# Transposing unscaled tokens by a product with a diagonal, in both RMS norms of a DeltaNet and MLP layer

## The chip, the cores and the metric

The kernel runs on one core of one Trainium2 chip. The metric is the time of one execution on the device in microseconds (us), as the median over several runs. A core has a matrix engine, TensorE (PE in the profile; PEld is its loading of weights), VectorE (DVE), ScalarE (ACT), GpSimd (POOL), and SyncE (SP), which here issues the transfers. Each engine works through its own queue of instructions in order, and semaphores order the engines among each other.

## The reference, cut to what matters

There is one layer of kind 0: a norm, a gated DeltaNet mixer, a residual add, a second norm, an MLP with squared ReLU, a residual add, and a final norm. The change touches the first two norms.

```
def rmsnorm(x, g):                                  # x: 1024 tokens x 1024
    y = x * rsqrt(mean(x * x, axis=-1) + 1e-6)      # one root for each token
    return y * g                                    # one gain for each column

h = x
h = h + gated_deltanet(rmsnorm(h, norm_mix_g), ...)   # (h @ w_in) -> conv, scan, ... -> @ w_out
h = h + square(relu(rmsnorm(h, norm_mlp_g) @ w1)) @ w2
out = rmsnorm(h, final_norm_g)
```

All data are 32-bit floats.

## The kernel before

The 1024 tokens are eight tiles of 128 (tokens on the partitions, 1024 columns free). A product with a weight matrix contracts over the columns, so the normed tokens are needed transposed, as `xT` for the mixer and `hT` for the MLP: 128 columns on the partitions for each of eight column blocks `kt`, tokens free. Both are kept as a high and a low half (`dh`, `dl`, a rounded value and what is left of it), since each big product is made of three products of 512 columns on rounded operands (lines 127 to 129, 824 to 826, 1080 to 1082, 1301 to 1303).

**First norm (lines 183 to 230).** For each tile, `norm_x` sums the squares (ACT or DVE, the squares go to a throw-away tile `junk`), adds the epsilon and takes the power -1/2 on POOL (lines 77 and 78), and scales the whole tile by its root in place (line 196; DVE for tiles 0 to 3, POOL for tiles 4 to 7). `turn_x` then transposes 128x128 blocks on TensorE against the identity (line 204) into eight PSUM tiles `tpx`, one for each `kt`, with four token tiles side by side in each. ACT writes the high half out of each and DVE the low half, both multiplied with the gain (lines 208 and 209). Tiles 0 to 3 (group 0) come first in the program; then `project_ab` (`pab`, a small product with `wab`) and the first window's products with the weights of key head 0 (`pk`, `half_of(0, 0)`). The squares of tiles 4 to 7 (group 1) are issued there, and their transposes after the first half of the second window (`half_of(1, 0)`, key head 1).

`tpv` (line 174) is the transpose of the small vectors (conv weights, gains), read from three small transfers into a tile `scr`; `pvec` is copied from it. Line 230 takes the exponential of `a_log`, eight numbers that a transfer (line 172) brings to all partitions; it is used much later, in `decays`.

**Second norm (lines 745 to 785, called at 833).** For each of the eight tiles of the output projection (products `pm`, lines 824 to 826), ACT sums the squares of the 1024 columns into `ss`, POOL takes the root, DVE multiplies the tile with root and gain into `hs` (line 751), and one tile later TensorE transposes `hs` (line 759) into two tiles `tpn`, out of which ACT and DVE write `hT` and sums that the MLP needs (`T1s`, `T2s`, `T4s`).

**Start of the MLP.** Each product of w1 with `hT` is done by a scheme of seven half-size products (`A11`, `S1` to `S4`, ... are sums of weight blocks; `T1`, `T2`, `T4` sums of `hT` blocks). Products 1 and 2 of the first three pairs come first (`p_0_1` to `p_2_2`), then `p_0_3`, `p_0_6`, `p_0_5`, ... `split_T` (lines 1021 to 1026) splits the T sums on ACT and DVE just before, under a higher priority; `wsplit` (line 83, `wh_S` in the trace) does the same for the weight sums.

The order on each engine is chosen by a list scheduler from priorities that follow the order of the program and from its own estimates of time; `tc.issue_after(x)` makes it hold instructions back until `x` has been issued. Tiles of one tag share a fixed number of buffers (`bufs`), in turn.

Of the kernel before, what the change touches and what calls it, by code (L numbers as in the profile page):

```python
# [28 lines left out]
def trunk_kernel(  # L29
# [144 lines left out]
    nc.tensor.transpose(tpv[:, 0:105], pv, ident[0:105, 0:105])  # L174


    nc.vector.tensor_scalar(out=pvec[:, 0:96], in0=tpv[:, 0:96], scalar1=0.5, scalar2=0.0, op0=MUL, op1=ADD)
    nc.vector.tensor_scalar(out=pvec[:, 96:97], in0=tpv[:, 96:97], scalar1=-0.5, scalar2=0.0, op0=MUL, op1=ADD)
    nc.vector.tensor_copy(pvec[:, 97:105], tpv[:, 97:105])
    sx = small([2, NT])  # L180

    def norm_x(t, sq, sc):

        junk = gp.tile([P, D], F32, tag="V", name=f"junk_{t}", bufs=2)
        ss = sx[:, 0, t : t + 1]
        if sq == "act":
            nc.scalar.activation(junk, xts[t], AF.Square, scale=1.0 / 32, accum_out=ss)
        else:
            nc.vector.scalar_tensor_tensor(out=junk, in0=xts[t], scalar=1.0 / D, in1=xts[t], op0=MUL, op1=MUL, accum_out=ss)
        rsqrt_pool(sx[:, 1, t : t + 1], ss, 1)  # L190
        rs = sx[:, 1, t : t + 1]
        if sc == "act":
            nc.scalar.activation(xts[t], xts[t], AF.Copy, scale=rs)
        else:
            eng = nc.gpsimd if sc == "pool" else nc.vector
            eng.tensor_scalar(out=xts[t], in0=xts[t], scalar1=rs, scalar2=1.0, op0=MUL, op1=MUL)

    def turn_x(g, tags):

        tps = [(ps if tag == "gemm" else px).tile([P, 512], F32, tag=tag, name=f"tpx_{g}_{kt}", bufs=4 if tag == "gemm" else 2)  # L200
               for kt, tag in enumerate(tags)]
        for kt, tp in enumerate(tps):
            for j in range(4):
                nc.tensor.transpose(tp[:, j * P : j * P + P], xts[4 * g + j][:, kt * P : kt * P + P], ident)
# [3 lines left out]
            nc.scalar.activation(dh, tp, AF.Copy, scale=gk)  # L208
            nc.vector.scalar_tensor_tensor(out=dl, in0=tp, scalar=gk, in1=dh.bitcast(F32), op0=MUL, op1=SUB)
# [22 lines left out]
    def decays():  # L232
        tab = px.tile([P, 512], F32, tag="ch", name="tab", bufs=2)
        for t in range(NT):
# [31 lines left out]
        nc.gpsimd.affine_select(out=up, in_=up, pattern=[[1, P]], compare_op=ALU.is_ge, fill=0.0,  # L266
                                base=0, channel_multiplier=-1)
# [225 lines left out]
    def merge(p, Xs):  # L493
# [7 lines left out]
        for e, (X, Y) in both:  # L501
# [3 lines left out]
            nc.gpsimd.memset(Y[0:32, :, 32:64], 0.0)  # L505
# [239 lines left out]
    def norm_to_T(src, t, g_bc, hs, name):  # L745

        ss = gp.tile([P, 2], F32, tag="sso", name=f"ss_{name}", bufs=3)
# [614 lines left out]
```

## Time and profile before

| | |
|---|---|
| median of 3 runs | 1277.77 us (1276.76 to 1277.99) |
| the profiled execution, its own time | 1277.02 us |
| its span on the core | 1275.3 us |
| TensorE busy | 1245.9 us, 98% |
| VectorE, ScalarE, GpSimd busy | 928.6, 734.6, 382.4 us |

The span is what the profile shows between the first and the last instruction; 1.7 us of the execution's own time lie around it. Busy times of TensorE overlap from one product to the next, since they are pipelined, so the step from one start to the next is what a product costs in a full queue.

### The profile page before, as it was taken

Reading aid. Unit: us, or ns where it says so; the run is one execution under the profiler, and the core shown is the slowest. Engines: PE = TensorE matmul, PEld = TensorE weight load, DVE = VectorE, ACT = ScalarE, POOL = GpSimd, SP = SyncE. Lnnn points to the kernel's source line nnn. Section 1 sums busy time; section 2 is a strip of 40 time slices with the busy share of each in tenths; the row PEclk is TensorE's granted clock in tenths of the full one; section 3 lists DMA queues with packets and bytes.
Section 4 is the critical chain, followed back from the end, with each engine's and each line's share of the span. In section 5 each row is a group of like instructions: output and inputs, shape, how many; then the busy total and the mean of one; then the engine's idle time right before and its main releaser. Section 6 shows DMA issues by size and latency. Waiting matters only on the chain. (4 is left out here: it accounts for less than half of the span.)

```text
span 1275.3 us, 18776 instructions
## 1 busy us (share of the span) xinstructions
PE 1245.9 (98%) x6656; PEld 1024.5 (80%) x6656; DVE 928.6 (73%) x1739; ACT 734.6 (58%) x1578; POOL 382.4 (30%) x335
## 2 busy tenths in 40 slices
PE   7999999999999999999999999999999999999996
PEld 5788888888888888778877888888887788888885
DVE  5799689679957976755657555555557997877897
ACT  4682465554565445643366554554558787686765
POOL 6120122111211101202234233233215444526484
PEclk9999999999999999999999999999999999999999
DMA  5241222221212120331153433333307225233003
GB/s 185 78 111 50 51 63 63 59 63 50 71 51 63 51 51 24 110 99 51 50 161 111 141 99 105 127 100 105 128 17 279 91 82 164 78 100 133 1 1 132
DMA packets 103983, 113.04 MB, mean 89 GB/s; under 512 B 23465, under 2 KB 75858, under 8 KB 103890
## 3 DMA queue, kind: packets, MB, share of 16 engines
q1 hardware_dynamic: 103890, 111.86, 28.3%
q8 instruction: 52, 0.85, 0.3%
q14 instruction: 41, 0.34, 0.1%
HBM read 90.83 MB, written 21.00 MB: 88 GB/s over the span
## 5 line engine op out<-in xcount | busy, mean ns | idle before, releaser
L1302 PE MATMUL p<-hT 128*128 128x512 f32 x448 | 174.9, 390 | 2.8 <-DVE hT L977 2.8
L1303 PE MATMUL p<-hT 128*128 128x512 f32 x448 | 174.3, 389 | 0.0
L1301 PE MATMUL p<-hT 128*128 128x512 f32 x448 | 173.7, 390 | 0.0
L954 POOL TENSOR_TENSOR u<-u,u 128x1024 f32<-128x1024 f32 x48 | 123.0, 2581 | 149.3 <-ACT cp_T L976 45.1
L975 ACT CAST hT<-u 128x1024 fp32r<-128x1024 f32 x112 | 112.8, 1050 | 29.5 <-PE p L1302 27.6
L78 POOL TENSOR_TENSOR sso<-sso,cons 128x1 f32<-128x1 f32 x64 | 42.1, 657 | 264.4 <-DVE sso L596 264.3
L1302 PEld LDWEIGHTS p<-hT 128*128 128x128 f32 x448 | 84.1, 188 | 22.0 <-DVE hT L977 4.5
L1301 PEld LDWEIGHTS p<-hT 128*128 128x128 f32 x448 | 84.1, 188 | 18.3 <-ACT P L1319 0.6
L1303 PEld LDWEIGHTS p<-hT 128*128 128x128 f32 x448 | 84.1, 188 | 17.2
L1104 DVE TENSOR_TENSOR u<-u,p 128x512 f32<-128x512 f32 x61 | 41.8, 686 | 44.6 <-PE p L1082 44.5
L1231 DVE TENSOR_TENSOR oT<-oT,p 128x512 f32<-128x512 f32 x80 | 53.1, 677 | 12.8 <-PE p L1303 12.8
L127 PE MATMUL pg<-xT,wh_g 128*128 128x512 f32 x128 | 54.4, 425 | 0.0
L127 PE MATMUL pq<-xT,wh_q 128*128 128x512 f32 x128 | 53.9, 421 | 0.0
L127 PE MATMUL pv<-xT,wh_v 128*128 128x512 f32 x128 | 53.6, 419 | 0.0
L127 PE MATMUL pk<-xT,wh_k 128*128 128x512 f32 x128 | 53.1, 415 | 0.0
L129 PE MATMUL pg<-xT,wl_g 128*128 128x512 f32 x128 | 52.4, 409 | 0.0
L128 PE MATMUL pg<-xT,wh_g 128*128 128x512 f32 x128 | 51.6, 403 | 0.0
L129 PE MATMUL pv<-xT,wl_v 128*128 128x512 f32 x128 | 51.6, 403 | 0.0
L128 PE MATMUL pv<-xT,wh_v 128*128 128x512 f32 x128 | 51.5, 402 | 0.0
L128 PE MATMUL pk<-xT,wh_k 128*128 128x512 f32 x128 | 51.1, 399 | 0.0
L824 PE MATMUL pm<-wh_o,oh 128*128 128x512 f32 x128 | 50.7, 399 | 0.3 <-ACT wh_o L83 0.2
L129 PE MATMUL pk<-xT,wl_k 128*128 128x512 f32 x128 | 50.9, 397 | 0.0
(319 smaller groups left out, 3630.1 us busy)
## 6 DMA issues: line engine op xcount, KB each, us to landing
u<-in_mlp_w_dram SPq DMA_DIRECT2D x38, 512.0 KB, 4.3
u<-hd SPq DMA_DIRECT2D x28, 512.0 KB, 5.0
ra<-in_mlp_w_dram SPq DMA_DIRECT2D x26, 512.0 KB, 4.2
hd<-u SPq DMA_DIRECT2D x25, 256.0 KB, 4.1
hd<-c SPq DMA_DIRECT2D x20, 256.0 KB, 2.3
xt<-in_x_dram SPq DMA_DIRECT2D x8, 512.0 KB, 4.7
wr_k<-in_gdn_w_in_dram SPq DMA_DIRECT2D x16, 256.0 KB, 3.3
wr_q<-in_gdn_w_in_dram SPq DMA_DIRECT2D x16, 256.0 KB, 2.9
```

What stands on the lines that cost most here:

```text
L78: nc.gpsimd.tensor_tensor(out=dst, in0=src, in1=mhalf[:, :n], op=ALU.pow)
L127: nc.tensor.matmul(o, hi, act[:, 0, kt, s], start=(kt == 0), stop=False)
L128: nc.tensor.matmul(o, hi, act[:, 1, kt, s], start=False, stop=False)
L129: nc.tensor.matmul(o, lo, act[:, 0, kt, s], start=False, stop=(kt == KT - 1))
L824: nc.tensor.matmul(o, oh[k // 4][0][:, k % 4, :], wo[k][0][:, s], start=(k == 0), stop=False)
L954: (V if name in ("T1", "T3") else G).tensor_tensor(out=o, in0=a, in1=b, op=op)
L975: nc.scalar.copy(hi, t)
L1104: add = lambda out, x, y: V.tensor_tensor(out=out, in0=x, in1=y, op=ADD)
L1231: add = lambda eng, out, x: eng.tensor_tensor(out=out, in0=out, in1=x, op=ADD)
L1301: nc.tensor.matmul(o, hid(0, kt)[:, s], w(0, kt), start=(kt == 0), stop=False)
L1302: nc.tensor.matmul(o, hid(0, kt)[:, s], w(1, kt), start=False, stop=False)
L1303: nc.tensor.matmul(o, hid(1, kt)[:, s], w(0, kt), start=False, stop=(kt == g - 1))
```

## The change

Both norms no longer scale before the transpose. In the first norm, POOL's root of a tile goes into a diagonal matrix `dx[:, t]` (identity times root, 128x128), and the transposes are ordinary products of the raw tile with this diagonal: out = tile^T times diag(root). The diagonals are made on DVE for tiles 0 to 3 and on POOL for tiles 4 to 7. In the second norm, `hs` is the tile times the gain alone (two halves, each right behind its add), the squares are summed in two halves, and the product is with `diag[:, t]`.

The steps of the first four tiles are put in a fixed order by `issue_after` (tile 0, 1, then the copies of `pvec`, tile 2, 3; tile 3's squares half on ACT, half on DVE). Group 0 is turned token tile by token tile over all eight `kt`, no longer `kt` by `kt`; group 1 is interleaved with the products of window 1's first half instead of following it.

```diff
-    def norm_x(t, sq, sc):
+    def square_x(t, sq):
...
+        if sq != "dve":
+            nc.scalar.activation(junk[:, lo], xts[t][:, lo], AF.Square, scale=1.0 / 32, accum_out=ss)
+        if sq != "act":
+            return nc.vector.scalar_tensor_tensor(out=junk[:, hi], in0=xts[t][:, hi], scalar=1.0 / D, in1=xts[t][:, hi], op0=MUL, op1=MUL,
+                                                  accum_out=s2 if sq == "both" else ss)
+
+    def norm_x(t, eng, sq=None):
+
+        ss, rs, s2 = (sx[:, i, t : t + 1] for i in range(3))
+        nc.gpsimd.tensor_scalar(out=ss, in0=ss, scalar1=s2 if sq == "both" else 0.0, scalar2=EPS, op0=ADD, op1=ADD)
+        root = rsqrt_pool(rs, ss, 1, 0.0)
+        return root, eng.tensor_scalar(out=dx[:, t, :], in0=ident, scalar1=rs, scalar2=1.0, op0=MUL, op1=MUL)
...
-        for kt, tp in enumerate(tps):
-            for j in range(4):
-                nc.tensor.transpose(tp[:, j * P : j * P + P], xts[4 * g + j][:, kt * P : kt * P + P], ident)
+        for j in range(4):
+            t = 4 * g + j
+            for kt, tp in zip(kts, tps):
+                nc.tensor.matmul(tp[:, j * P : j * P + P], xts[t][:, kt * P : kt * P + P], dx[:, t, :], start=True, stop=True)
...
-    for t, (sq, sc) in enumerate((("act", "dve"), ("dve", "dve"), ("act", "dve"), ("act", "dve"))):
-        norm_x(t, sq, sc)
-
-    split(wab[:, :, 0:16], wab[:, :, 16:32], rab, "pool", "pool")
-    split(*wt0[0], raw0[0], "act")
-    split(*wt0[1], raw0[1], "pool", "pool")
-    turn_x(0, ["gemm"] * 4 + ["tp", "ch"] * 2)
+    square_x(0, "act")
+    square_x(1, "dve")
+    rooted, normed = norm_x(0, nc.vector)
+    with tc.issue_after(rooted.ins):
+        rooted, normed = norm_x(1, nc.vector)
+    with tc.issue_after(normed.ins):
...
+        square_x(2, "act")
+        squared = square_x(3, "both")
+    with tc.issue_after(squared.ins), tc.issue_after(rooted.ins):
+        norm_x(2, nc.vector)
+        rooted, normed = norm_x(3, nc.vector, "both")
+
+    with tc.issue_after(rooted.ins), tc.issue_after(normed.ins):
+        split(wab[:, :, 0:16], wab[:, :, 16:32], rab, "pool", "pool")
+        split(*wt0[0], raw0[0], "act")
+        split(*wt0[1], raw0[1], "pool", "pool")
+    turned = turn_x(0, range(KT), lambda kt: "gemm" if kt < 4 else ("tp", "ch")[kt % 2])
     project_ab(0)
     nc.scalar.activation(nea, nea, AF.Exp)
...
-    half_of(0, 0, plan[0])
-    for t, (sq, sc) in enumerate((("act", "pool"), ("dve", "pool"), ("act", "pool"), ("dve", "pool"))):
-        norm_x(4 + t, sq, sc)
-    half_of(1, 0, None)
-    turn_x(1, ["tp", "ch"] * 4)
+    with tc.issue_after(turned[0].ins), tc.issue_after(turned[1].ins):
+        half_of(0, 0, plan[0])
+        for t, sq in enumerate(("act", "dve", "act", "dve")):
+            square_x(4 + t, sq)
+            norm_x(4 + t, nc.gpsimd)
+    half_of(1, 0, [[lambda kt=kt: turn_x(1, [kt], lambda kt: ("tp", "ch")[kt % 2])] for kt in range(KT)])
...
-        nc.scalar.activation(hs, src, AF.Square, scale=1.0 / 32, accum_out=ss[:, 0:1])
-        rsqrt_pool(ss[:, 1:2], ss[:, 0:1], 1)
-        yield
-        nc.vector.scalar_tensor_tensor(out=hs, in0=src, scalar=ss[:, 1:2], in1=g_bc, op0=MUL, op1=MUL)
+        for n in range(2):
+            c = slice(n * 512, n * 512 + 512)
+            nc.scalar.activation(pt[n], src[:, c], AF.Square, scale=1.0 / 32, accum_out=ss[:, n : n + 1])
+            nc.vector.tensor_tensor(out=hs[:, c], in0=src[:, c], in1=g_bc[:, c], op=MUL)
+        nc.gpsimd.tensor_scalar(out=ss[:, 2:3], in0=ss[:, 0:1], scalar1=ss[:, 1:2], scalar2=EPS, op0=ADD, op1=ADD)
+        rsqrt_pool(ss[:, 3:4], ss[:, 2:3], 1, 0.0)
+
+        dg = diag[:, t, :]
+        nc.vector.tensor_scalar(out=dg, in0=ident, scalar1=ss[:, 3:4], scalar2=1.0, op0=MUL, op1=MUL)
+        yield
...
-                nc.tensor.transpose(tp[:, j * P : j * P + P], hs[:, kt * P : kt * P + P], ident)
+                nc.tensor.matmul(tp[:, j * P : j * P + P], hs[:, kt * P : kt * P + P], dg, start=True, stop=True)
```

How the queues come out of it, at three places. **ACT at the start of the program**, before the change: `tpx_6` and `tpx_7` are the last two of group 0's evacuations, L187 the squares of tiles 4 and 6, and L230 is the exponential of `a_log` (its tile is one of the small ones in `scr`).

```order
L208 ACTIVATE xT<-tpx_6_165,pvec 128x512
L208 ACTIVATE xT<-tpx_7_166,pvec 128x512
L187 ACTIVATE junk_271,scr_94<-xt_117 128x1024
L187 ACTIVATE junk_281,scr_94<-xt_121 128x1024
L220 COPY abT<-pab_215 32x512
L230 ACTIVATE scr_94<-scr_94 128x8
L305 ACTIVATE kT_442<-pk_0_234,pvec 128x512
```

The same queue of the changed kernel, from the squares of tiles 2 and 3 on (L185, the second one now half a tile):

```order
L185 ACTIVATE junk_144,scr_94<-xt_101 128x1024
L185 ACTIVATE junk_146,scr_94<-xt_106 128x512
L83 CAST wh_k_0_108<-wr_k_0_110 128x512
L247 ACTIVATE scr_94<-scr_94 128x8
L209 ACTIVATE xT<-tpx_0_161,pvec 128x512
L209 ACTIVATE xT<-tpx_1_162,pvec 128x512
```

The exponential (now L247) has moved from behind all eight evacuations of group 0 to the place ahead of the first of them.

**TensorE around group 1**, before: the end of window 1's first half (`pk_0_291`) and the first transposes (`xt_117` to `xt_123` are token tiles 4 to 7).

```order
L127 MATMUL pk_0_291<-xT,wh_k_1_244 128x512
L128 MATMUL pk_0_291<-xT,wh_k_1_244 128x512
L129 MATMUL pk_0_291<-xT,wl_k_1_245 128x512
L204 MATMUL tpx_0_316<-ident,xt_117 128x128
L204 MATMUL tpx_0_316<-ident,xt_119 128x128
L204 MATMUL tpx_0_316<-ident,xt_121 128x128
L204 MATMUL tpx_0_316<-ident,xt_123 128x128
```

After, from the end of window 0's first half (`pk_0_236`) on:

```order
L128 MATMUL pk_0_236<-xT,wh_k_1_112 128x512
L129 MATMUL pk_0_236<-xT,wl_k_1_113 128x512
L204 MATMUL tpx_0_294<-dx,xt_117 128x128
L204 MATMUL tpx_0_294<-dx,xt_119 128x128
L204 MATMUL tpx_0_294<-dx,xt_121 128x128
L204 MATMUL tpx_0_294<-dx,xt_123 128x128
L127 MATMUL pk_0_293<-xT,wh_k_0_240 128x512
L128 MATMUL pk_0_293<-xT,wh_k_0_240 128x512
L129 MATMUL pk_0_293<-xT,wl_k_0_241 128x512
L204 MATMUL tpx_1_304<-dx,xt_117 128x128
```

The first four products of group 1 now stand ahead of window 1's first half (24 products earlier), four for each three of its products.

**ACT at the start of the MLP**, before: the splits of T1 and T4 (`cpT`, `T1h`, `T4h`), the relu and square of the first results, and the weight sums S4, S2, S1 of pair 0.

```order
L83 CAST wh1_0_S4_6812<-u1_6690 128x512
L1021 COPY cpT1_1_6862<-T1s_5916 128x1024
L1025 CAST T1h_6717<-cpT1_0_6861 128x1024
L1025 CAST T1h_6717<-cpT1_1_6862 128x1024
L1097 ACTIVATE c11_1_6829<-c11_1_6829 128x512
L1021 COPY cpT4_0_6891<-T4s_5918 128x1024
L83 CAST wh1_0_S2_6843<-s2_0_6808 128x512
L1021 COPY cpT4_1_6892<-T4s_5918 128x1024
L1025 CAST T4h_6718<-cpT4_0_6891 128x1024
L1025 CAST T4h_6718<-cpT4_1_6892 128x1024
L1108 COPY u7_6696<-p1_2_1_6847 128x512
L83 CAST wh1_0_S1_6870<-s1_0_6807 128x512
```

After:

```order
L1053 CAST T1h_6744<-cpT1_0_6888 128x1024
L1053 CAST T1h_6744<-cpT1_1_6889 128x1024
L1122 ACTIVATE c11_1_6856<-c11_1_6856 128x512
L1049 COPY cpT4_0_6918<-T4s_5920 128x1024
L1125 ACTIVATE c11_1_6856<-c11_1_6856 128x512
L1049 COPY cpT4_1_6919<-T4s_5920 128x1024
L1053 CAST T4h_6745<-cpT4_0_6918 128x1024
L1053 CAST T4h_6745<-cpT4_1_6919 128x1024
L83 CAST wh1_0_S2_6870<-s2_0_6835 128x512
L1136 COPY u7_6723<-p1_2_1_6874 128x512
L83 CAST wh1_0_S1_6897<-s1_0_6834 128x512
```

The cast of S2, which `p_0_6` needs, now stands behind all of T4's split instead of in the middle of it; three 1024-column operations have gone ahead of it. On TensorE, one product of `p_0_5` (with S1) has moved in behind the second product of `p_0_6`, and the last tile's `tpn` products stand six products earlier.

## Rows read from the trace of the kernel before

**Rows 1.** The page's busy times of each engine (share of span) and instructions.

```profile
PE 1245.9 (98%) x6656; PEld 1024.5 (80%) x6656; DVE 928.6 (73%) x1739; ACT 734.6 (58%) x1578; POOL 382.4 (30%) x335
```

**Rows 2.** Waits of TensorE: line, releaser, us in total, times, longest.

```profile
PE tpv L174 <- DMA scr<-in_gdn_conv_w_dram: 8.3, 1, 8.3
...
PE tpn_h L759 <- DVE hs L751: 1.6, 2, 0.8
PE tpkk L376 <- ACT tpk L367: 1.2, 1, 1.2
```

**Rows 3.** Groups on TensorE: records, busy us, mean ns, idle before.

```profile
L376 PE MATMUL tpkk<-kT 128*128 128x128 f32 x128 | 19.9, 277 | 1.2 <-ACT tpk L367 1.2
...
L204 PE MATMUL tpx<-ident,xt 128*128 128x128 f32 x64 | 10.9, 323 | 0.9 <-DVE xt L196 0.7 <-POOL xt L196 0.2
```

**Rows 4.** TensorE's timeline, 90 to 94 us: start, duration, operation, count.

```profile
90.71 1.05 PE L433 MATMUL tpqk<-conv_q,kT 128*128 128x128 f32 x8
...
91.83 0.40 PE L128 MATMUL pv<-xT,wh_v 128*128 128x512 f32 x1
92.06 0.40 PE L129 MATMUL pv<-xT,wl_v 128*128 128x512 f32 x1
92.31 0.66 PE L321 MATMUL tpq<-ident,conv_q 128*128 128x128 f32 x4
...
93.04 0.39 PE L128 MATMUL pv<-xT,wh_v 128*128 128x512 f32 x1
```

**Rows 5.** The timeline of all engines, 9 to 30 us.

```profile
9.64 0.25 DVE L177 TENSOR_SCALAR pvec<-tpv 128x96 f32<-128x96 f32 x1
...
11.27 0.45 SPq L172 DMA_DIRECT2D scr<-in_gdn_a_log_dram  x1
...
11.54 4.14 PE L204 MATMUL tpx<-ident,xt 128*128 128x128 f32 x24 [0.43 <-DVE xt L196]
...
12.86 0.73 POOL L85 TENSOR_SCALAR wab<-scr 128x128 fp32r<-128x128 f32 x1
...
14.19 4.74 ACT L208 ACTIVATE xT<-tpx,pvec 128x512 fp32r<-128x512 f32 x8 [3.03 <-PE tpx L204]
14.91 5.36 DVE L209 SCALAR_TENSOR_TENSOR xT<-tpx,pvec,xT 128x512 fp32r<-128x512 f32 x8 [0.78 <-ACT xT L208]
...
16.97 0.39 PE L127 MATMUL pk<-xT,wh_k 128*128 128x512 f32 x1
...
22.04 0.20 ACT L230 ACTIVATE scr<-scr 128x8 f32<-128x8 f32 x1
...
24.71 0.69 DVE L88 TENSOR_TENSOR wl_k<-wr_k,wh_k 128x512 fp32r<-128x512 f32 x1
...
29.28 0.57 POOL L78 TENSOR_TENSOR scr<-scr,cons 128x1 f32<-128x1 f32 x1
```

**Rows 6.** Group 0's transposes (L204) by stretch: ns min/median/max, first and last start.

```profile
L204 PE MATMUL tpx<-ident,xt x4: 417/417/417, 13.3 to 13.9; 128*128 128x128 f32 x4
...
L204 PE MATMUL tpx<-ident,xt x5: 272/273/273, 15.0 to 15.4; 128*128 128x128 f32 x5
```

**Rows 7.** The transfer of `a_log` (L172), from its issue to its landing.

```profile
DMA to landing us min/median/max: 5.8/5.8/5.8
```

**Rows 8.** The timeline of DVE, PE and ACT, last tile of the second norm and first splits.

```profile
647.95 1.28 DVE L751 SCALAR_TENSOR_TENSOR hs<-oT,ss_h,gx 128x1024 f32<-128x1024 f32 x1 [1.71 <-POOL ss_h L78]
...
649.38 1.06 PE L759 MATMUL tpn_h<-ident,hs 128*128 128x128 f32 x8 [0.84 <-DVE hs L751]
...
666.85 0.62 ACT L83 CAST wh_S<-s 128x512 fp32r<-128x512 f32 x1
667.36 1.02 ACT L1021 COPY cpT<-T4s 128x1024 f32<-128x1024 f32 x1
...
667.52 0.50 PE L1080 MATMUL p<-T2h,wh_S 128*128 128x512 f32 x1 [1.46 <-ACT wh_S L83]
...
668.31 1.93 ACT L1025 CAST T4h<-cpT 128x1024 fp32r<-128x1024 f32 x2
```

More of the change, by code (lines that the diff above doesn't have):

```diff
@@ L198, in turn_x @@
-    def turn_x(g, tags):
-        tps = [(ps if tag == "gemm" else px).tile([P, 512], F32, tag=tag, name=f"tpx_{g}_{kt}", bufs=4 if tag == "gemm" else 2)
-               for kt, tag in enumerate(tags)]
-        for kt, tp in enumerate(tps):
-            for j in range(4):
-                nc.tensor.transpose(tp[:, j * P : j * P + P], xts[4 * g + j][:, kt * P : kt * P + P], ident)
+    sx = small([3, NT])
+    dx = gp.tile([P, NT, P], F32, tag="kk", name="dx", bufs=NKK)
+    def square_x(t, sq):
+        junk = gp.tile([P, D], F32, tag="V", name=f"junk_{t}", bufs=2)
+        ss, s2 = sx[:, 0, t : t + 1], sx[:, 2, t : t + 1]
+        lo, hi = (slice(0, 512), slice(512, 1024)) if sq == "both" else (slice(0, D),) * 2
+        if sq != "dve":
[3 more added lines that the diff above has]
+                                                  accum_out=s2 if sq == "both" else ss)
@@ new lines, in norm_x, with turn_x @@
+    def norm_x(t, eng, sq=None):
[3 more added lines that the diff above has]
+        return root, eng.tensor_scalar(out=dx[:, t, :], in0=ident, scalar1=rs, scalar2=1.0, op0=MUL, op1=MUL)
+    def turn_x(g, kts, tag):
+        tps = [(ps if tag(kt) == "gemm" else px).tile([P, 512], F32, tag=tag(kt), name=f"tpx_{g}_{kt}", bufs=4 if tag(kt) == "gemm" else 2)
+               for kt in kts]
+        for j in range(4):
+            t = 4 * g + j
+            for kt, tp in zip(kts, tps):
+                nc.tensor.matmul(tp[:, j * P : j * P + P], xts[t][:, kt * P : kt * P + P], dx[:, t, :], start=True, stop=True)
+        for kt, tp in zip(kts, tps):
@@ L207, in turn_x @@
             gk = pvec[:, 97 + kt : 98 + kt]
-            nc.scalar.activation(dh, tp, AF.Copy, scale=gk)
-            nc.vector.scalar_tensor_tensor(out=dl, in0=tp, scalar=gk, in1=dh.bitcast(F32), op0=MUL, op1=SUB)
+            high = nc.scalar.activation(dh, tp, AF.Copy, scale=gk)
+            low = nc.vector.scalar_tensor_tensor(out=dl, in0=tp, scalar=gk, in1=dh.bitcast(F32), op0=MUL, op1=SUB)
+        return high, low
     abT = gp.tile([P, T], F32, tag="sg", name="abT", bufs=1)[0:32, :]
@@ L265, in decays @@
         nc.gpsimd.memset(up, 1.0)
[L266 to L267 removed]
+        with tc.issue_after(rooted.ins):
+            nc.gpsimd.affine_select(out=up, in_=up, pattern=[[1, P]], compare_op=ALU.is_ge, fill=0.0,
+                                    base=0, channel_multiplier=-1)
         nc.vector.tensor_scalar(out=up[0:64, :], in0=up[0:64, :], scalar1=-1.0, scalar2=0.0, op0=ADD, op1=ADD)
@@ L810, in trunk_kernel @@
         wo.append(load_wrow(w_out[k * P : k * P + P, :], f"o{k}", "act", gp, t2))
+    diag = gp.tile([P, NT, P], F32, tag="conv", name="diag", bufs=3)
     for t in (0, 1, 4, 5, 2, 6, 3, 7):
@@ L832, in trunk_kernel @@
         hs = gp.tile([P, D], F32, tag="dm", name=f"hs{t}", bufs=2)
-        later.append(start(norm_to_T(acc, t, gx, hs, f"h{t}")))
+        later.append(start(norm_to_T(acc, t, pt, gx, hs, f"h{t}")))
     finish()
```

28 lines of the change are left out of this document (8 added, 20 removed).

## The prediction

> **What bounds the kernel now.** I read the page's busy times first. TensorE is busy for 98% of the span and every other engine for 73% or less [rows 1], so a part of the change pays only where TensorE waits, and each thing that it adds to TensorE's queue is paid nearly in full. So I next read what TensorE waits for: 8.3 us at the start for the small vectors' transfer, 1.6 us in two waits for `hs` of the second norm, 1.2 us in one wait for ACT in the scan's stage [rows 2]. Of these only the 1.6 us is a wait on work that the change shortens. The third view is the one that decides: what a transpose costs on TensorE, and what a plain product of two 128x128 float tiles costs.
>
> **Transpose against product.** The program makes 64 products `tpkk` (8 heads, 8 chunks), and the trace has 128 records of them; it makes 64 transposes `tpx`, and the trace has 64 [rows 3]. A plain float product is two records, a transpose one. What a record costs in a full queue: eight records of `tpqk` (four products) take 1.05 us, one alone about 0.275, so seven steps take 0.78 us, 0.11 each [rows 3, 4]; eight transposes take 1.06 us, one alone 0.273, so again 0.11 each [rows 6, 8]. From the neighbours: from the first `tpqk` at 90.71 to the second 512-column product behind it at 91.83, less one such product (0.23, the step from 91.83 to 92.06), four products take 0.89 us, 0.22 each; in the same way four transposes from 92.31 to 93.04 take 0.50 us, 0.125 each [rows 4]. So a product with the diagonal costs 0.10 to 0.11 us more than the transpose that it replaces. I take 0.11. The change replaces 64 + 64 of them. The Trainium skill would make it worse: its page "TensorE: Matmul & The Clock Gate", section "Terms", gives the transpose mode of trn2 as four times faster for FP32. By that a product would cost an estimated 0.45 us, 0.33 more than a transpose, and the sum below would be some 21 us higher. The trace does not agree: `tpkk` has two records for a product, not four, and the sum goes by the rows.
>
> **Start, group 0 (32 products).** Before, the transposes end at 15.7 us, ACT's evacuations run from 14.19 and DVE's from 14.91 to 20.27, and `pk` starts at 16.97 behind five `pab` products of 0.23, so the full queue effectively begins at 15.83 [rows 5]. From there TensorE does not wait until group 1.
> - The products cannot start before the small vectors land at 8.3 either, since `tpv` stands ahead of them [rows 2]. The scaling of tiles (four on DVE) drops out, and the first diagonals are made by about 8 us (0.25 for 128x96 on DVE [rows 5]), so TensorE is full from 8.5 us on.
> - The transposes up to about 14 us took 417 ns each, those behind took 273 [rows 6]. The windows view prints a granted clock of 1.00 over both, but I read the lengths as its lower and its upper level, 1.2 and 2.4 GHz, after nearly 6 us of transposes with gaps. If the clock rises at the same time, 5.8 us hold 27 records at 0.21, and the other 37 of the 64 take 4.1 us: the products end at 18.4. If a fuller queue lifts it at about 11 us, they end at 16.8.
> - In either case a new wait ties the start: the exponential of `a_log` now stands ahead of the first evacuation in ACT's queue (the change's first place). Its transfer is issued at 11.27 and lands 5.8 us later [rows 5, 7], at 17.1. Before, it was done at 22.04, long after landing. Queued behind it are the eight evacuations, for which DVE and then `pab` wait. So: 17.1 + 0.2 for the exponential, 0.6 for a high half, 0.67 for a low half (each an eighth of [rows 5]'s 4.74 and 5.36), first `pab` at 18.7 against 15.83: **+2.9 us**. Lower bound, if the transfer lands early and the clock rises early: 16.8, +1.0. Upper, landing a microsecond later beside the token tiles: +3.9.
>
> **Group 1 (32 products).** +32 x 0.11 = **+3.5 us**, all in a full queue. Moving them ahead of window 1's first half takes their slack: before, a scaled tile was 0.2 us late; now tile 7's diagonal is needed 24 products earlier. DVE's chain from its last low half (20.27) to the low half of `wl_k` at 25.40 is 5.1 us [rows 5]. The changed order puts tile 7's squares one operation before its end, so they are done 4.4 us after the low halves' end, now at 18.0 + 5.4 = 23.4: 27.8. Then the add and the power on POOL (0.57 for the power, no more for the add) and the diagonal there, which no row shows: 0.3 to 0.73 (a 128x128 operation on POOL [rows 5]). 28.9 to 29.7, I take 29.0. TensorE comes to tile 7 after 40 products of 0.23 from 18.7 and three of 0.22: 28.5. **+0.5** (0 to +1.2), less the **0.2** of the old transposes' wait for POOL [rows 3], which goes. Behind that the pieces of window 1 need one evacuation in each 1.6 us, which ACT (0.6) and DVE (0.67) can give.
>
> **Scan's stage.** Its 1.2 us wait for ACT [rows 2] may shrink, since TensorE comes later and the evacuations of group 1 are spread over window 1: **-0.6** (-1.2 to 0).
>
> **Second norm (64 products).** In tiles 1 to 6 no wait on `hs` is listed, so nothing is gained and 48 x 0.11 = **+5.3 us** is paid. Tile 0 pays 0.9 and wins back about 0.75 of its wait [rows 2]: **+0.15**. Its 1.28 us scaling becomes a 0.25 us diagonal, and behind the last add stands a square of 512 columns (0.59, as an evacuation) and no more one of 1024 (1.02, as a copy of that width), so the products are ready 1.4 us sooner [rows 5, 8]. DVE's and ACT's additional halves lie beside 11 us of products in each tile. Tile 7 is as much sooner, but its products stand six products (1.4 us) earlier, so its wait stays at 0.7 of 0.84, and the passes cost 0.9. Behind it TensorE waits 1.46 us for the cast of S2 at 667.52 [rows 8]. ACT's order now has the second copy and both casts of T4 ahead of that cast (0.95 from 667.36 to 668.31, and 1.93 [rows 8]): 2.8 us later. ACT starts that chain 1.2 us sooner and TensorE comes 0.75 later, so the wait grows by about 0.9. The waits behind it, for S1 and for low halves (some 0.75 listed), come due meanwhile and mostly go. Tile 7 and the splits: **+0.9** (-0.6 to +3.5).
>
> **The sum.** 2.9 + 3.5 + 0.5 - 0.2 - 0.6 + 5.3 + 0.15 + 0.9 = +12.4 us. On the profiled execution's own 1277.02 (span 1275.3 and 1.7 around it) that is 1289.4. That execution lies 0.75 under the median of the runs, inside their spread, and I keep 1289.4 as the forecast. The lower bounds together (with 0.10 for a product) give about +6.5, the upper ones +18; they don't come together, and the likeliest case spans 1285 to 1293.
>
> **The rivals.**
> - *The splits lose more.* S2 and S1 both wait behind T4's split, the one product of `p_0_5` that moved into `p_0_6` holds the queue until S1's cast, and nothing is made up: +3.5 instead of +0.9, with a late landing of `a_log`: 1293 to 1296. For it: the order at the third place. Against it: the low halves of S2 come from DVE anyway, so part of that time was waited before too. 8 in 100.
> - *The waits give more back.* The clock rises early, the transfer lands early, the 1.2 us and the splits' waits go: +6.5 to +8, 1283.5 to 1285. 7 in 100.
> - *Not slower: a product with a diagonal costs one record.* Then the terms with 0.11 vanish, and the start (tied by `a_log`), the 0.3 of group 1, -0.6, -0.75 of tile 0 and about 0 at the splits leave +1.8 or less: 1277 to 1278.8. It decides from the point where a product costs less than 0.02 us more than a transpose. Against it: `tpkk` and `tpqk`, with different operands, both come in two records for a product [rows 3, 4]. 5 in 100.
> - *A product holds TensorE for four records.* 96 products then cost 96 x 0.33 = 32 us and not 10.6, and group 0 (32 x 0.45 = 14.3 us at the upper clock, from 8.5 on) ends at 23 or later and not before 18.7: about 1315. Against it: each plain product of the kernel shows two records. 1 in 100. This is what the rule of the Trainium skill above would do here.
>
> **How the numbers follow.** The likeliest case has 78 in 100 between 1285 and 1293, and its middle is the forecast. The range for 8 in 10 is 1284.5 to 1293.2; it takes in the edges of the two neighbours. A change within 0.2% (2.6 us) is about what a measurement of this kernel cannot tell from none. Only the one-record rival ends there, with 3 within and 2 faster of its 5, and 1 more each for what I have not seen: faster 0.03, same 0.04, slower 0.93.
>
> **What would show it.** In the changed profile: 128 more records on TensorE (6784), with `tpx` and `tpn` at 128 each; `tpx` records of 0.42 us up to 11 to 14 us; the exponential on ACT ending at 17.1 to 17.4 with ACT idle before it, and `pab` starting at 18.5 to 18.8; a wait of `tpx` on POOL's `dx` near 28.5; no wait on `diag` but at the last tile; a wait of `p_0_6` for S2 of 2 us or more. Wrong would be: `tpx` and `tpn` at 64 records, or steps of 0.06 between their records; `pab` at 16 us; or a wait that I don't name, above all behind `pab` or in the splits, of more than 2 us.

## The result, and the profile after

The changed kernel takes 1298.18 us, median of 4 runs (1297.82 to 1299.56), beside 1277.88 us for the kernel before (4 runs, 1276.76 to 1280.11). The ratio is 1.0157 [1.0145, 1.017]: slower, as forecast, but by 20.3 us and not by 12.4; the time lies 5 us above the range. The profiled execution has 1298.40 us with a span of 1296.2, against 1277.02 with 1275.3.

The page of the changed kernel, busy times and the clock that TensorE was granted in 40 slices (answers to [rows 1]):

```profile
span 1296.2 us, 19066 instructions
...
PE 1264.0 (98%) x6784; PEld 1043.3 (80%) x6784; DVE 936.9 (72%) x1757; ACT 736.3 (57%) x1594; POOL 383.6 (30%) x335
...
PEclk9999999999999999999999999999999999999998
```

TensorE has the 128 more records that two for each product give, and is still the bound at 98%. At this grain the clock looks full; it was not, as shown below.

The groups of the two transposed norms on TensorE (records, busy us, mean ns, idle before; answers to [rows 3]):

```profile
L204 PE MATMUL tpx<-dx,xt 128*128 128x128 f32 x128 | 18.1, 297 | 2.2 <-POOL dx L195 2.2
L786 PE MATMUL tpn_h<-diag,hs 128*128 128x128 f32 x128 | 16.3, 283 | 2.5 <-DVE diag L777 2.5
```

What TensorE waited for (total us, times, longest; answers to [rows 2]):

```profile
PE tpv L174 <- POOL scr L193: 8.1, 1, 8.1
PE p L1108 <- ACT wh_S L83: 3.6, 2, 3.3
PE p L1330 <- DVE hT L1005: 2.5, 3, 1.4
PE tpn_h L786 <- DVE diag L777: 2.5, 2, 2.0
PE tpx L204 <- POOL dx L195: 2.2, 2, 1.4
PE pab L220 <- DVE xT L210: 1.5, 1, 1.5
```

The wait for `hs` became one for `diag`, and longer (2.5 us against 1.6); `dx` costs 2.2 us and S2's cast (`wh_S`) 3.3; the wait of `tpkk` for ACT is gone.

To place the loss I took the start of one and the same product of TensorE in both traces (the n-th record of a product that the change leaves alone) and subtracted, at marks along the program. The difference grows by:

| Stretch | Forecast | Measured |
|---|---|---|
| start, up to the first `pab` | +2.9 | +3.13 |
| group 1 | +3.5 +0.5 -0.2 | +5.85 |
| scan's stage, to the first output products | -0.6 | -1.6 |
| second norm, tile 0 | +0.15 | +0.7 |
| tiles 1 to 6 | +5.3 | +5.5 |
| tile 7 and the splits of T1, T2, T4 | +0.9 | +3.8 +2.4 |
| behind them, near 985 us | 0 | +1.0 |
| whole | +12.4 | +20.8 |

Two stretches make most of the miss, and the clock has a part in the second. First group 1, the timeline of POOL, DVE and TensorE (start, duration, operation, idle time before):

```profile
23.49 1.80 POOL L78 TENSOR_TENSOR scr<-scr,cons 128x1 f32<-128x1 f32 x1
...
23.65 1.22 DVE L187 SCALAR_TENSOR_TENSOR junk<-xt 128x1024 f32<-128x1024 f32 x1
...
25.39 1.72 POOL L195 TENSOR_SCALAR dx<-ident,scr 128x128 f32<-128x128 f32 x1
...
25.73 1.22 DVE L187 SCALAR_TENSOR_TENSOR junk<-xt 128x1024 f32<-128x1024 f32 x1
...
29.98 0.71 PE L204 MATMUL tpx<-dx,xt 128*128 128x128 f32 x4 [1.44 <-POOL dx L195]
...
30.32 0.57 POOL L78 TENSOR_TENSOR scr<-scr,cons 128x1 f32<-128x1 f32 x1
...
30.98 0.38 POOL L195 TENSOR_SCALAR dx<-ident,scr 128x128 f32<-128x128 f32 x1
...
31.42 0.49 PE L204 MATMUL tpx<-dx,xt 128*128 128x128 f32 x2 [0.73 <-POOL dx L195]
```

The same power takes POOL 0.57 us when DVE is elsewhere and 1.80 beside a 1024-wide square of DVE; the same diagonal 0.38 and 1.72. These two long ones belong to tile 4, the first of the four that POOL serves in turn. The squares of tile 7 end at 26.95, but POOL is at tiles 5 and 6 until 29.92, and so the last diagonal is ready at 31.36, where I had 29.0. The conflict was there in the kernel before, in the timeline of [rows 5]:

```profile
20.18 1.22 DVE L189 SCALAR_TENSOR_TENSOR junk<-xt 128x1024 f32<-128x1024 f32 x1
...
20.36 1.47 POOL L78 TENSOR_TENSOR scr<-scr,cons 128x1 f32<-128x1 f32 x1
```

Second, tile 7 of the second norm, the timeline of POOL and DVE:

```profile
659.40 1.62 POOL L1225 TENSOR_TENSOR oT<-oT 128x512 f32<-128x512 f32 x1 [10.90 <-ACT wh_A L83]
...
659.79 1.78 DVE L772 TENSOR_TENSOR hs<-oT,gx 128x512 f32<-128x512 f32 x1
...
661.12 0.62 POOL L773 TENSOR_SCALAR ss_h<-ss_h 128x1 f32<-128x1 f32 x1
661.82 0.56 POOL L78 TENSOR_TENSOR ss_h<-ss_h,cons 128x1 f32<-128x1 f32 x1
662.42 0.28 DVE L777 TENSOR_SCALAR diag<-ident,ss_h 128x128 f32<-128x128 f32 x1 [0.85 <-POOL ss_h L78]
```

POOL's subtraction `oT` (L1225, L1197 in the kernel before) stood behind the scaling with the root before, since it overwrites a half of the tile that the scaling reads:

```profile
649.32 1.68 POOL L1197 TENSOR_TENSOR oT<-oT 128x512 f32<-128x512 f32 x1 [1.40 <-DVE hs L751]
```

Now that half is read early, at 652.00 (`hs`), and the subtraction goes right behind the tile's last add (659.27), ahead of the root's add and power. It also holds DVE up: the product `hs`, which takes 0.69 us elsewhere, starts 0.39 us behind the subtraction, takes 1.78 and ends 0.55 us after it. TensorE waits 2.04 us for `diag` (0.84 for `hs` before [rows 8]).

The granted clock of this part is the third view. The windows of the same trace (us, busy us of each engine, PEclk, DMA):

```profile
600.00:664.00 64.00, 61.96 (x317) 52.30 (x316) 40.40 (x57) 20.03 (x43) 19.22 (x19) 1.00 0.17 52
664.00:667.50 3.50, 3.50 (x14) 3.02 (x14) 2.73 (x5) 1.69 (x3) 0.00 (x0) 0.51 1.03 350
667.50:688.00 20.50, 16.91 (x73) 13.21 (x71) 12.64 (x14) 17.89 (x26) 8.44 (x6) 1.00 0.52 165
688.00:691.40 3.40, 3.39 (x9) 2.54 (x9) 3.40 (x4) 2.26 (x5) 3.05 (x3) 0.50 0.03 11
691.40:984.90 293.50, 292.12 (x1282) 240.03 (x1281) 167.14 (x221) 159.42 (x256) 86.35 (x60) 1.00 0.33 104
984.90:988.30 3.40, 3.40 (x10) 2.63 (x9) 3.27 (x3) 1.27 (x3) 3.32 (x2) 0.50 1.02 402
```

Before the last microseconds the clock is at its lower level (0.5, 1.2 GHz) in three stretches, each behind a wait of TensorE: behind the 2.04 us for `diag`, behind 3.32 + 0.27 us for the casts of S2 and S1, and behind 1.38 us for `hT` of the second layer. In them products of 512 columns start 0.43 us apart and not 0.23, so each stretch gives away up to 1.7 us. In the trace before, the clock is full from 14.3 to 1270 us.

### The profile page after: what moved, and what is told of

Read it like the earlier page. It is cut to its first block, busy times and chain, and to the rows that moved or that the text cites. A ratio compares the mean times of both kernels' runs of the same rounds, so it can differ in the third digit from the quotient of the medians.

```text
span 1296.2 us, 19066 instructions
## 1 busy us (share of the span) xinstructions
PE 1264.0 (98%) x6784; PEld 1043.3 (80%) x6784; DVE 936.9 (72%) x1757; ACT 736.3 (57%) x1594; POOL 383.6 (30%) x335
## 5 line engine op out<-in xcount | busy, mean ns | idle before, releaser
L1005 DVE TENSOR_TENSOR hT<-cp_S,hT 128x1024 fp32r<-128x1024 f32 x32 | 39.1, 1222 | 16.5 <-ACT hT L1003 14.0
```

Of the source, the lines that this page charges most:

```text
L1005: V.tensor_tensor(out=lo, in0=cp, in1=hi.bitcast(F32), op=SUB)
```

## The experiments

Theory: the change costs what its second records cost, plus waits of its new order, each of which can be mended by itself, plus the clock behind them. Rivals: the products themselves (a smaller or larger price, or a lower clock under them), or waits that only hand their time on. "Behind" below means that one instruction is kept after another in its engine's queue.

**The exponential of `a_log` behind the last of group 0's evacuations.** (`turned[0]` is the high half of the last `kt`. The runs below that use the same edit put it there too, where their expectations say "the first".)

```diff
+    with tc.issue_after(turned[0].ins):
+        nc.scalar.activation(nea, nea, AF.Exp)
```

> The changed kernel, with the exponential of a_log held behind the last of group 0's evacuations on ACT; nothing else moves in any queue. Theory: the first pab waits 1.49 us at 18.93 because ACT sat until 17.22 on the transfer of a_log. Then pab starts at about 17.4, when the products of group 0 end, and everything behind it shifts: 1.4 us less, about 1296.8. Rival: the start is bound by the products at the lower clock or by DVE; then pab stays at 18.5 or later, and the time stays within 0.4 us of 1298.2.

1297.9 us, ratio 1.0152 [1.0137, 1.0168], where 1296.8 was expected. `pab` starts 1.05 us earlier and does not wait, but group 1 then waits 2.5 us for `dx`, the 2.04 us in front of tile 7 are followed by a full clock, and S2's cast is awaited for 4.82 us, with 6.8 us at the lower level from 685.0. The wait is what I said; its time is taken back. The other 2.1 us of the start are the products themselves.

**Group 1's products behind window 1's first half.**

```diff
-    half_of(1, 0, [[lambda kt=kt: turn_x(1, [kt], lambda kt: ("tp", "ch")[kt % 2])] for kt in range(KT)])
+    half_of(1, 0, None)
+    for kt in range(KT):
+        turn_x(1, [kt], lambda kt: ("tp", "ch")[kt % 2])
```

> The changed kernel, with group 1's products put back behind the first half of window 1, as before the change. Theory: the two waits of tpx for POOL's dx (2.2 us) come only from the place in TensorE's queue; they go, and the stretch of group 1 costs 3.5 us for the second records alone: 2.2 us less, about 1296. Rival: the waits move elsewhere (the evacuations of group 1 then stand together in front of pab, or the scan's stage loses the 1.25 us that it gave back): less than 1 us.

1294.96 us, ratio 1.0132 [1.0117, 1.0147]. No wait for `dx` is left, and group 1 costs 3.0 us and not 5.85: the move of these products, not their price, made the excess there. The time fell by 3.2 us and not by the 2.2 expected; this profile also lacks the fall of the clock near 985 us, though the wait there (1.39 us) stayed.

**POOL's subtraction behind the same tile's root.**

```diff
-                        G.tensor_tensor(out=acc_of(4, m), in0=acc_of(4, m), in1=acc_of(7, m), op=SUB)
+                        with tc.issue_after(roots[4 + m].ins):
+                            G.tensor_tensor(out=acc_of(4, m), in0=acc_of(4, m), in1=acc_of(7, m), op=SUB)
```

> The changed kernel, with each of POOL's four subtractions of oT held behind the root of its own token tile; nothing but POOL's queue changes. Theory with the clock: the wait of 2.04 us on tile 7's diagonal shrinks to about 0.7, and the clock stays at its upper level there (no products of 0.43 us spacing behind it): 1.3 + 1.7 = 3 us less, about 1295.2. Theory without the clock (it falls there whatever TensorE waits): 1.3 us less, about 1296.9, with the slow products still behind tile 7. Rival: S2's cast bounds what follows anyway and grows by as much: within 0.5 us of 1298.2.

1299.12 us, ratio 1.0162 [1.0147, 1.0177]. The wait for `diag` stays at 1.93 us. The timeline says why:

```profile
661.71 0.56 POOL L78 TENSOR_TENSOR ss_h<-ss_h,cons 128x1 f32<-128x1 f32 x1
...
662.24 1.26 POOL L1228 TENSOR_TENSOR oT<-oT 128x512 f32<-128x512 f32 x1
662.30 1.27 DVE L779 TENSOR_SCALAR diag<-ident,ss_h 128x128 f32<-128x128 f32 x1 [0.85 <-POOL ss_h L78]
```

Now the subtraction starts 0.06 us ahead of the diagonal, which takes 1.27 us in place of 0.28 and ends with it. My theory of the order alone falls; it is order and sharing. The Trainium skill's page "SBUF — State Buffer", section "SBUF: two separate sides", says that DVE, in a two-port mode or with two inputs in SBUF, and GpSimd share one pair of ports as an exclusive lock, which the one that starts first holds for the whole instruction. These rows agree: the later one ends 0.07 us behind the earlier one here, and 0.55 at 659.79 in the changed kernel.

**The subtraction behind the same tile's last POOL step of the splits.**

```diff
+                        with tc.issue_after(fourths[4 + m].ins): G.tensor_tensor(out=acc_of(4, m), in0=acc_of(4, m), in1=acc_of(7, m), op=SUB)
```

> The changed kernel with POOL's subtraction of 128x512 (sum of the first layer's accumulators) issued behind the same tile's last POOL step of the splits, so that nothing of 128x512 runs on POOL beside the tile's own scaling and diagonal on DVE. Theory (the two engines slow each other: hs 1.78 us beside the subtraction in the changed kernel, diag 1.27 us beside it where it was held behind the root): both go back to 0.69 and 0.28, the wait for tile 7's diagonal from 2.04 to 0.95 us, the clock does not fall there; 1298.2 - 1.1 - 1.7 = 1295.4 us. Rival (order of POOL alone counts, or the wait lies with the add and power): wait stays at 1.9 us, time 1297.5 to 1299.5 us.

The timeline of DVE and TensorE at tile 7 and the splits:

```profile
659.55 0.69 DVE L772 TENSOR_TENSOR hs<-oT,gx 128x512 f32<-128x512 f32 x1
...
661.08 0.29 DVE L777 TENSOR_SCALAR diag<-ident,ss_h 128x128 f32<-128x128 f32 x1 [0.84 <-POOL ss_h L78]
...
661.51 2.02 PE L786 MATMUL tpn_h<-diag,hs 128*128 128x128 f32 x16 [0.94 <-DVE diag L777]
...
685.60 0.80 PE L1108 MATMUL p<-T2h,wh_S 128*128 128x512 f32 x1 [5.25 <-ACT wh_S L83]
```

`hs` and `diag` are back at 0.69 and 0.29, the wait is 0.94, the clock stays full there, and tile 7 costs 1.06 us and not 3.8. But S2's cast comes only 1.0 us sooner and TensorE 3.0: the wait for it grows to 5.25, with the clock at its lower level from 685.5. What ACT does between the tile and that cast starts with T2's first copy, in the kernel before and in this run:

```profile
655.83 1.02 ACT L1021 COPY cpT<-T2s 128x1024 f32<-128x1024 f32 x1 [0.19 <-DVE hT L784]
```

```profile
670.24 1.02 ACT L1049 COPY cpT<-T2s 128x1024 f32<-128x1024 f32 x1 [2.04 <-DVE hT L811]
```

That is 6.45 us behind the first product of tile 7 before and 8.73 here (8.85 in the changed kernel): ACT waits for `hT`, and DVE now makes one more low half of weights (`wl_A`) ahead of it. So the splits are late even with the tile on time. The median is 1298.47 us, ratio 1.0163 [1.0146, 1.018], and not the 1295.4 expected; the profiled execution has 1295.26, the other three 1298.4 to 1298.8 with a lower mean clock (0.994 beside 0.996). Mechanism shown, gain not kept.

**T4's copies behind S2's cast on ACT.**

```diff
-                with tc.high_priority(offset=40):
+                with tc.high_priority(offset=40), tc.issue_after(casts["0_S2"]) if pos == 5 else nullcontext():
```

> The changed kernel with T4's copies and casts on ACT queued behind S2's cast, which in it stands behind them (five ACT instructions, 4.2 us from 681.69). Theory (the wait of 3.3 us and the fall of the clock behind it come from that place in ACT's queue, which the scheduler chose): wait 0 to 1.2 us (S1's cast then follows T4's), clock full there: 1298.2 minus 2.1 to 3.3 minus 1.7 = 1293.2 to 1294.4 us. Rival (the lateness comes with tile 7, and the next operand is late instead): wait moves to S1's cast or T1's halves at about 2 us or more, and 1297 us or above.

1295.35 us, ratio 1.014 [1.0124, 1.0155]. S2's wait is gone, S1's is 1.45 us, the clock is full at the splits (not behind tile 7, nor near 983 us), and they give back 1.3 us where they had cost 2.4. The microsecond missing to the expected time lies mostly in the scan's stage, which in this profile gave back 0.6 and not 1.6.

**One norm at a time.** The changed kernel with the second norm of before, then with the first norm of before:

```diff
-                nc.tensor.matmul(tp[:, j * P : j * P + P], hs[:, kt * P : kt * P + P], dg, start=True, stop=True)
+                nc.tensor.transpose(tp[:, j * P : j * P + P], hs[:, kt * P : kt * P + P], ident)
...
-                nc.tensor.matmul(tp[:, j * P : j * P + P], xts[t][:, kt * P : kt * P + P], dx[:, t, :], start=True, stop=True)
+                nc.tensor.transpose(tp[:, j * P : j * P + P], xts[4 * g + j][:, kt * P : kt * P + P], ident)
```

> The changed kernel with the second norm as before (tokens scaled, then transposed); only the first norm's part of the change is left. Theory (the parts add up as the offsets in the changed kernel's trace say): +9.0 us at the end of group 1, -1.6 over the scan, then nothing at the norm tiles, at tile 7 and at the splits, where the waits are again 0.84 and 1.5 us: 1277.9 + 7.4 = 1285.3 us. Rival (part of what is lost at tile 7 and the splits comes from the first norm, by the order that the scheduler then gives): 1287 to 1289 us.

> The kernel before with the second norm of the changed one. Theory: start and group 1 as before, tiles 0 to 6 +6.2 us, tile 7 and the splits +4 to +6.2 (diagonal's wait 2.0, S2's cast 3 us or more, one or two falls of the clock), up to +1.0 behind them: 1277.9 + 10.2 to 13.4 = 1288.1 to 1291.3 us; with the run above the two parts then add up to the change. Rival (tile 7 and the splits lose only together with the first norm): 1285 us.

1286.09 us, ratio 1.0063 [1.005, 1.0077], with the old waits of 0.84 and 1.42 us back; and 1290.89, ratio 1.01 [1.0084, 1.0115], with 2.04 us for `diag` and 4.81 for S2. The two losses, 7.8 and 12.6 us over that call's 1278.25, make 20.5, beside the change's 20.3: the norms lose independently. In the second, the clock stayed full behind the same 2.04 us for `diag`.

**Transposes in place of the products, in the changed order.** The diagonals are replaced by ones, so the multiplication with the roots is left out. The line of the second norm is shown; that of the first is changed likewise.

```diff
-                nc.tensor.matmul(tp[:, j * P : j * P + P], hs[:, kt * P : kt * P + P], dg, start=True, stop=True)
+                nc.tensor.transpose(tp[:, j * P : j * P + P], hs[:, kt * P : kt * P + P], dg)
```

> The changed kernel, with TensorE's transpose in place of the product in both norms, and with the diagonals made by an operation of the same size and the same inputs that gives ones, so that every dependency and TensorE's whole order stay as they are; the multiplication with the roots is left out. Theory: the second record of each product costs 0.11 us where the queue is full, 96 times: 10.6 us less, about 1287.6, with tpx and tpn at 64 records each, and the start still tied to a_log. Rival: the waits and the clock make most of the 20 us, and the records little: 1294 or more. Four records' worth for a product (0.33) is excluded if less than 15 us go.

1291.85 us, ratio 1.0103 [1.0086, 1.012], 4 us above the expected time: 6.3 of the 20.3 us go. The timeline of TensorE in it, tile 7's eight transposes (with products they are the line with 16 records above):

```profile
658.56 1.06 PE L786 MATMUL tpn_h<-diag,hs 128*128 128x128 f32 x8 [2.04 <-DVE diag L777]
```

One record each, 0.96 us less for eight. Tiles 1 to 6 then cost nothing (0.0 against 5.5 us), so the second record is the whole of that term. A transpose takes about half the time of a product (1.06 against 2.02 us for eight). By the page of the Trainium skill that the prediction names, "TensorE: Matmul & The Clock Gate", section "Terms", it would be a quarter; the rows do not agree. The waits for `dx`, `diag` and S2 all stay. At the start it even loses: `pab` waits 5.0 us for its low half, and the clock is at its lower level from 15.8 to 22.6 us. It falls three times more, near 33, 681 and 978 us, with no product with a diagonal in the kernel.

**All four queues at once** (exponential, group 1, subtraction behind T4's steps, S2 ahead), with the products kept:

> The changed kernel with four queues mended at once: the exponential of a_log behind the first evacuation, group 1's products behind window 1's first half, POOL's subtraction behind T4's steps, S2's cast ahead of T4's. The products with a diagonal stay. Theory (what is left are the second records of the products): 1277.9 + 3.5 + 3.5 + 7.2 for the records, - 1.4 for the first tiles' queue, - 1.3 of the scan stage = 1289.4 us, granted clock full but for at most one fall (1.7 us): 1288.5 to 1291.2 us. Rival (the waits are not independent: each one mended hands its time to the next): 1293 us or more.

1291.88 us, ratio 1.0107 [1.0092, 1.0122]. Between the two expectations: waits of 1.03 us (S2) and 1.61 (S1) are left, and stretches at 685.6 and 979.2 us at the lower clock, the second behind 1.38 us for `hT`. So:

**The same with S1's cast ahead too.**

```diff
+                with tc.high_priority(offset=40), tc.issue_after(casts["0_S1"]) if pos == 5 else nullcontext(), tc.issue_after(casts["0_S2"]) if pos == 5 else nullcontext():
```

> The changed kernel with the four queues mended as in the run with all of them, and S1's cast ahead of T4's copies too. There the waits of the splits were 1.03 (S2) and 1.61 us (S1), and behind them the clock fell for 3.4 us. Theory (what is left without these waits are the second records of the products): S2's wait about 0.5 us, no wait of 1 us for S1, clock full at the splits; 1291.9 - 1.7 - 0.8 = 1289.4 us. Rival (the lower clock belongs to the products or to the splits, not to waits): the fall stays and the time with it, 1291 us or more.

1287.76 us, ratio 1.0075 [1.0061, 1.0088]. The timeline of TensorE in it, at tile 7 and the splits:

```profile
658.70 2.02 PE L789 MATMUL tpn_h<-diag,hs 128*128 128x128 f32 x16 [0.94 <-DVE diag L780]
...
678.53 0.50 PE L1111 MATMUL p<-T2h,wh_S 128*128 128x512 f32 x1 [1.02 <-ACT wh_S L83]
```

and its windows:

```profile
14.00:1270.00 1256.00, 1246.22 (x6722) 1029.09 (x6721) 920.69 (x1724) 727.32 (x1577) 365.36 (x303) 1.00 0.28 84
```

The clock is full from 14 to 1270 us, also behind a wait of 1.02. Only the stretch at 685 went with its wait, though; the 1.38 us for `hT` are still there, and that the clock stayed full behind them was luck, which is part of why this run is 1.6 us below the expected time. By stretches: start +1.6, group 1 +3.0, scan -0.3, tile 0 +0.7, tiles 1 to 6 +5.5, tile 7 +1.0, splits -0.9, in all +10.7 in the profile. What is left is little more than the second records and the start.

**Is a wait enough to lower the clock?** The kernel before, all transposes, with one and then three extra multiplications on POOL ahead of tile 7's root (they change only scratch):

```diff
+        if t == 7:
+            nc.gpsimd.tensor_tensor(out=hs[:, 0:512], in0=hs[:, 0:512], in1=src[:, 0:512], op=MUL)
```

> The kernel before with one POOL multiplication of 128x512 more, ahead of tile 7's add and power, so that tile 7's product with the norm has to wait longer (0.84 us now); the output is the same, since what it multiplies is scratch. It tests in the kernel before, without any diagonal, what a longer wait does. Theory A (a wait of about 2 us in front of the first product of the second stage is enough for the granted clock to fall to its lower level for some microseconds behind it): wait 2.2 to 2.5 us, clock 0.5 for 3.4 us, time 1277.9 + 1.5 + 1.7 = 1281.1 us. Theory B (the falls in the changed kernel come from the products with a diagonal, not from the wait): the wait alone, 1279.4 us, clock full.

> The kernel before, all transposes, with three POOL multiplications of 128x512 ahead of tile 7's add and power (one of them took 1.3 us and moved the wait from 0.84 to 1.75 us, and the profile showed no fall). Theory (a wait of TensorE is enough, without any product with a diagonal): wait 4.4 us, granted clock 0.5 for some us behind it, 1278.2 + 3.6 + 1.7 = 1283.5 us. Rival (only the changed kernel's products let it fall): clock full, 1281.8 us.

With one: wait 1.75 us (2.2 to 2.5 expected), full clock in the profile, 1280.3 us, ratio 1.0014 [1.0004, 1.0023]. Of its ten executions five with a mean clock of 0.998 average 1278.9 us and five with 0.995 or 0.996 average 1281.4: something fell in half of them, which their means alone do not place. With three: 1283.89 us, ratio 1.0049 [1.0036, 1.0062]. The timeline of TensorE at the wait:

```profile
657.02 1.94 PE L763 MATMUL tpn_h<-ident,hs 128*128 128x128 f32 x8 [3.42 <-DVE hs L755]
```

and the windows around it:

```profile
640.00:655.50 15.50, 13.60 (x64) 10.97 (x62) 5.47 (x8) 4.71 (x8) 4.82 (x5) 1.00 0.36 110
655.50:660.00 4.50, 2.98 (x11) 2.77 (x12) 2.35 (x3) 1.17 (x2) 1.33 (x2) 0.62 0.62 212
```

Behind 3.42 us of waiting the eight transposes take 1.94 us and not 1.06, the clock being at 0.5 for 3.4 us from 656.6. There is no product with a diagonal in this kernel: a wait is enough. (This profile has a second such stretch at 66.1 us, behind 2.02 us of waiting in the scan's stage.)

The traces of all sixteen profiles bear on which wait does it. Between 14 and 1270 us the clock fell 23 times, each time during or shortly behind a wait of TensorE of 1.35 us or more. All nine waits of 3.3 us or more came with a fall. Of six waits of 2.04 us in front of the same product, tile 7's with `diag`, three did (the changed kernel and the runs with group 1 behind and with S2 ahead), and three did not (the exponential behind, the transposes, the first norm of before). Of the 1.38 us for `hT` near 980 us, which every profile has, five of sixteen did.

**Towards a faster kernel.** The change's queue by tile with scaled tokens and transposes, the mended queues and S2 and S1 ahead; and the kernel before with S2 and S1 ahead alone (the same edit as in the run with S1 above). Of the first:

```diff
+        return root, eng.tensor_scalar(out=xts[t], in0=xts[t], scalar1=rs, scalar2=1.0, op0=MUL, op1=MUL)
...
+                nc.tensor.transpose(tp[:, j * P : j * P + P], xts[t][:, kt * P : kt * P + P], ident)
```

> A version that keeps the change's queue by tile for tiles 0 to 3, and transposes scaled tokens as before (also in the second norm): the exponential of a_log behind the first evacuation, group 1's products behind window 1's first half, S2's and S1's casts ahead of T4's copies. Theory (queue by tile is worth 0.9 us, since tile 3's scaling ends at 12.5 instead of 13.4 us, and S2's wait of 1.5 us about 1.0): 1277.9 - 1.9 = 1276.0 us, 0.15% faster than before. Rival (the start is bound by the transposes and the evacuations of all four tiles, not by tile 3's scaling): 1277 us, or slower where a wait moves.

> The kernel before with T4's copies on ACT queued behind the casts of S2 and S1. Theory (the waits of 1.46 and 0.27 us lie in ACT's order alone): S2's wait 0.2 to 0.5 us, S1's none: 1277.9 - 1.2 = 1276.7 us, 0.1% faster. Rival (S1's cast then waits for its buffer, or T4's halves come late for their product): no change, 1277.5 to 1278.5 us.

1277.52 us, ratio 0.9993 [0.9985, 1.0002], and 1277.5, ratio 0.9996 [0.9987, 1.0004]. Neither can be told from the kernel before. In the first the transposes end at 15.0 us and `pab` starts 0.56 later than before, since it now waits 1.33 us for POOL's low half of `wab`: the gain of the queue by tile goes into the next wait. In the second S2's wait falls from 1.46 to 0.51 us, inside the scatter.

## Why the prediction was wrong

**Direction and mechanism of the records: right.** Two records for a product, 128 in all more. Eight products take 0.98 us longer than eight transposes (2.02 against 1.04 to 1.06), 0.12 each; tiles 1 to 6 cost 5.5 (5.3 forecast), and with transposes nothing.

**The start: right.** Forecast +2.9 and `pab` at 18.7; measured +3.13 and 18.93. The exponential stands ahead of the evacuations and waits for `a_log` (behind them it saves 1.05 us; the rest is the products):

```profile
17.22 0.21 ACT L247 ACTIVATE scr<-scr 128x8 f32<-128x8 f32 x1 [6.45 <-DMA scr<-in_gdn_a_log_dram]
17.34 4.72 ACT L209 ACTIVATE xT<-tpx,pvec 128x512 fp32r<-128x512 f32 x8
...
18.93 1.33 PE L220 MATMUL pab<-xT,wab 128*32 128x512 f32 x5 [1.49 <-DVE xT L210]
```

**Group 1: mis-sized.** I had the operations (squares, add, power, diagonal) and the place of the wait right, and took the durations from an idle POOL: 0.57 for the power, at most 0.73 for the diagonal. Beside DVE's squares they are 1.80 and 1.72, and the wait 2.2 and not 0.5. I also let tile 7's chain start at the end of its own squares; these came sooner than I had them (26.95, not 27.8), and POOL's queue of tiles 4 to 6 decided. The timeline of [rows 5] has the same conflict in the kernel before (1.47 us at 20.36); I had read a short operation of it.

**Tile 7 and the splits: the step that failed.** "Tile 7 is as much sooner ... so its wait stays at 0.7 of 0.84" takes POOL to be free for the root. The subtraction that had been held by the scaling was released by the change and ran ahead of it: 2.04 us. I costed what the change issues, and not what it no longer holds back. "So the wait grows by about 0.9" became 1.9 (3.32 against 1.46): the order on ACT was read rightly, but "ACT starts that chain 1.2 us sooner" was not. Tile 7 came later, and from its first product to T2's first copy it takes 8.85 us and not 6.45. With tile 7 alone mended, that tile costs 1.06, but the chain is still 8.73 us behind it and S2's wait is 5.25. With tile 7, S2 and S1 mended, the tile and the splits together cost 0.15.

**The clock: absent from the sum.** I gave the lower level a place at the start only. Three stretches behind 1.4 to 3.6 us of waiting cost up to 1.7 each, by estimate some 4 of the 8.4 us that the measured offsets in the table lie above the sum (1.6 at tile 7, which is 3.8 less 0.98 for the records and 1.2 for the wait; up to 1.7 at the splits; 1.0 near 985 us). That a wait can do it is shown by the kernel before with a longer one, and that it does not need the products by the run with transposes. The rival "the splits lose more" (1293 to 1296) named the order at the splits; its price lacked the clock and tile 7, and the measured time lies above it too.

**Smaller terms.** The scan's stage gave back 1.6 and not 0.6: the 1.2 of `tpkk` went whole, and the rest is not traced. Tile 0 cost 0.7 and not 0.15, since a wait of 0.5 us for `diag` is left there. The bounds listed in the prediction add up to about +7 and +17.4, not +6.5 and +18; the measured +20.8 lies outside either way.

Which of the waits between 1.35 and 2.04 us lower the clock stays open: 1.38 us at 984.3 did in the profile of the changed kernel, 1.39 us at the same place did not before. Executions of one kernel differ by 2 to 3 us, in part with their mean clock. So a part of what a single profile shows, and of what a single run gained or lost, is luck. Whether the `a_log` transfer could land earlier wasn't tried.

## What to carry to other kernels

When a change removes a wait, list what that wait was holding back on every engine, and where the released instruction now stands: here it was a subtraction that nobody had touched. Take a duration on POOL or DVE from a row where the other does what it will do beside it, not from the shortest row. On a TensorE that is 98% busy, price a new wait at its length and, as these traces have it, a wait of 3 us or more again for a stretch at the lower clock (1.7 us here), one of 2 us for half the chance of it. Mend the waits together, since one mended alone often handed its time to the next.

## What the runs showed of the hardware that was not expected

- DVE and POOL can hold each other up for most of an instruction of the other: a DVE product of 0.69 us became 1.78, a DVE diagonal of 0.28 became 1.27, a POOL power on 128 numbers 0.57 became 1.80.
- TensorE's clock at half level for 3.4 us (6.8 in two runs) during or behind a wait of 1.4 to 5.3 us, in a kernel that keeps it 98% busy. The same wait does not always do it: 2.04 us in front of one product did in three of six profiles, 1.38 us in front of another in five of sixteen.
- A product of 128x128 floats costs 0.12 us more than a transpose of the same data: eight transposes are 8 records in 1.06 us, eight products 16 in 2.02.
